# Gate weights laid out in memory by groups of expert blocks instead of blocks of tokens

## The chip, the cores and the metric

The kernel runs on one core of one Trainium2 chip. The metric is the device time of one execution in microseconds (us). The kernel before has a median of 3892.26 us over three runs (3888.90 to 3899.44 us).

## The reference, cut to what matters

Two layers, each with a token mixer, a cross-attention and a product-key expert layer (PEER); 512 tokens, 1024 channels. The change lies in the PEER layer: 16384 single-neuron experts, of which each token uses 128 (8 heads, the best 16 of each).

```
idx   = (e1 * 128 + e2)                # 128 experts a token
gates = softmax(vals)                  # their weights
ub  = peer_u[idx];  act = gelu(einsum('tkd,td->tk', ub, x))
vb  = peer_v[idx];  out = einsum('tk,tkd->td', gates * act, vb)
```

## The kernel before, in words

For 384 of the 512 tokens (TD) the kernel computes all experts densely and weights them by a gate that is zero for an expert that the token did not choose. The 16384 experts are 128 blocks (j) of 128 (n), and a group (GRP) is 8 blocks. The other 128 tokens fetch their own 128 rows of U and of V with indirect DMAs of GpSimd (`rows` L779, `rv` L795), in the same two stages:

- Stage U: for each block j a 128x1024 weight `w` is loaded (L198), split into a rounded part `wh` (ScalarE, L200) and a rest `wl` (VectorE, L202), and 24 matmuls of 384 columns give `acc` (L216 to L218). Its Gelu goes to `ag` and, four blocks at a time, to `acts` in memory (L1029). The last two groups stay in the core. Meanwhile the routing of the tokens is worked out, and for every 4 tokens `spread` and `collect` make a 128 (expert n) x 128 (block j) table of gates in PSUM and copy it into `stage`. A stage holds 16 tokens (TB): on each partition n, 128 blocks x 16 tokens of float32. When it is full it is written to `gd` (printed `gates`, L994 and L997): 24 writes of 1 MB a layer.
- Stage V: the blocks are taken by groups, the last group first. At a group's first block, the gates `gg` of the whole group are loaded (L807, 24 token blocks x 8 blocks x 16 tokens on each partition, 1.5 MB), then the activations `ar` of the group (L1058, 1.5 MB). The loads for a group are called for ahead, as soon as the buffer of that parity is free: two buffers of each. Then per block: `wv` = activation x gate (VectorE, L1062), its split `ws` (L222, L223), and 24 matmuls into eight accumulators `out` in PSUM. The first group's gates have a place of their own, `big`, and are loaded at the end of stage U, after all 24 writes have landed.

All loads and stores but the indirect ones are issued by SyncE in program order, on one queue (q1). GpSimd's are on another (q0). `w` has 4 buffers (WB), `wh` 3 (HB), `wl` 3 (LB); `stage` 2; `rows` 3 and `rv` 4. The order of the instructions on each engine follows the program's generators (`routes`, `scatter`, `rows_u`, `rows_v`), which are advanced by fixed credits for each block.

In memory, `gd` before is [24 token blocks, 128 n, 128 j, 16 tokens]. A stage is 8192 contiguous bytes on each partition, so a write is 128 packets of 8192 bytes. A group's gates are, for each n and token block, 8 x 16 x 4 = 512 contiguous bytes, so a read is 3072 packets of 512 bytes, 1 MiB apart from one token block to the next.

Of the kernel before, what the change touches and what calls it, by code (L numbers as in the profile page):

```python
# [10 lines left out]
F32 = mybir.dt.float32  # L11
# [14 lines left out]
NK = 128  # L26
# [6 lines left out]
TB = 16  # L33
TD = 384
NTB = TD // TB
# [15 lines left out]
GRP = 8  # L51
# [102 lines left out]
def trunk(ctx: ExitStack, tc: tile.TileContext, A, out, dbg=None):  # L154
    nc = tc.nc
# [13 lines left out]
    @contextmanager  # L169
    def tpool(**kw):  # L170
        if kw.get("space") == bass.MemoryType.DRAM:
            with tc.tile_pool(**kw) as pool:
                yield pool
        else:
            with tc.tile_pool(reuse_waits="tile", **kw) as pool:
                yield pool if kw.get("space") == PS else Lines(pool)
# [5 lines left out]
    dram = ctx.enter_context(tpool(name="dram", bufs=1, space=bass.MemoryType.DRAM))  # L182
# [577 lines left out]

    def peer(l):
        acts = dram.tile([NK // GRP, 128, GRP, TD], F32, name=f"acts{l}")
        gd = dram.tile([NTB, 128, NK, TB], F32, name=f"gates{l}")
        NG = T // 128 - TD // 128
        left = ExitStack()
        gp = left.enter_context(tpool(name=f"pg{l}", bufs=1))
# [36 lines left out]
        gates = {}  # L803

        def gate_group(pool, name, g):
            gg = pool.tile([128, NTB, GRP, TB], F32, name=name)
            nc.sync.dma_start(gg, gd[:, :, g * GRP:(g + 1) * GRP, :].rearrange("b p j t -> p b j t"))  # L807
            return gg

        with tpool(name=f"pr{l}", bufs=1) as rt, tpool(name=f"ph{l}", bufs=1) as hp, tpool(name=f"pps{l}", bufs=4, space=PS) as psum, \  # L810
# [132 lines left out]
            def spread(t0):  # L943
                parts = t0 // 4 % GVM < GVN
                dt = F32R if parts else F32
                oh = pp.tile([128, 8, NK], dt, name="oab", bufs=2)
                nc.vector.tensor_tensor(oh, C("iota")[:, None, :].to_broadcast([128, 8, NK]),  # L947
                                        pe[:, t0:t0 + 4].rearrange("p t e -> p (t e)")[:, :, None]
                                        .to_broadcast([128, 8, NK]), op=OP.is_equal)
                ob = pp.tile([128, 4, 2, NK] if parts else [128, 4, 1, NK], dt, name="ob", bufs=2)  # L950
                for i in range(4):
                    for k in ((0, 1) if parts else (2,)):
                        nc.scalar.activation(ob[:, i, k % 2], oh[:, 2 * i + 1].bitcast(F32), AF.Copy,  # L953
                                             scale=pg[:, k, t0 + i:t0 + i + 1])
                return oh, ob, parts

            def collect(t0, oh, ob, parts, stage):
                dst = stage[:, :, t0 % TB:t0 % TB + 4]
                if parts:
                    for h in range(2):  # L960
                        g = psm.tile([128, 2, 2, NK], F32, name="sm")
                        for i in range(2):
                            nc.tensor.matmul(g[:, i], lhsT=oh[:, 4 * h + 2 * i], rhs=ob[:, 2 * h + i], start=True,  # L963
                                             stop=True)
                        d = dst[:, :, 2 * h:2 * h + 2]
                        nc.scalar.copy(d, g[:, :, 0].rearrange("p t n -> p n t"))
                        nc.vector.tensor_add(d, g[:, :, 1].rearrange("p t n -> p n t"), d)
                else:
                    g = psm.tile([128, 4, NK], F32, name="sm")
                    for i in range(4):  # L970
                        nc.tensor.matmul(g[:, i], lhsT=oh[:, 2 * i], rhs=ob[:, i, 0], start=True, stop=True)  # L971
                    nc.scalar.copy(dst, g.rearrange("p t n -> p n t"))

            routed = [False] * TT

            def routes():
                for t in RORD:
                    yield from route(t)
                    routed[t] = True

            def scatter():
                for t in range(TD // 128):
                    pend = None
                    for t0 in range(t * 128, (t + 1) * 128, 4):
                        while not routed[t]:
                            yield
                        if t0 % TB == 0:
                            stage = pp.tile([128, NK, TB], F32, name="stage", bufs=2)
                        cur = (t0,) + spread(t0) + (stage,)
                        yield  # L990
                        if pend:
                            collect(*pend)
                            if t0 % TB == 0:
                                nc.sync.dma_start(gd[t0 // TB - 1], pend[-1])  # L994
                        pend = cur
                    collect(*pend)
                    nc.sync.dma_start(gd[(t + 1) * 128 // TB - 1], pend[-1])  # L997
                gates[NK // GRP - 1] = gate_group(gp, "big", NK // GRP - 1)

            rows = rows_u() if NG else iter(())  # L1000
            todo, groups = routes(), scatter()
            last = []
            rc = gc = xc = 0.0
# [37 lines left out]
        with tpool(name=f"pv{l}", bufs=1) as vp, tpool(name=f"vps{l}", bufs=1, space=PS) as psum:  # L1041
            acc = [psum.tile([128, T], F32, name=f"out{c}") for c in range(DC)]
            pend = []
# [8 lines left out]
            for j in v_order():  # L1052
                g, i = divmod(j, GRP)
                if i == 0:
                    gg = gates.get(g) or gate_group(vp, f"gg{g % 2}", g)
                    if j < NK - GC * GRP:
                        ar = vp.tile([128, GRP, TD], F32, name=f"ar{(g + 1) % 2}")
                        nc.sync.dma_start(ar, acts[g])  # L1058
                kept = j - (NK - GC * GRP)
                act = ar[:, i] if kept < 0 else last[kept // 4][:, i % 4]  # L1060
                wv = vp.tile([128, TD], F32, name="wv", bufs=2)
                nc.vector.tensor_mul(wv.rearrange("p (b t) -> p b t", b=NTB),  # L1062
                                     act.rearrange("p (b t) -> p b t", b=NTB), gg[:, :, i, :])
                ws = vp.tile([128, 2, TD], F32R, name="ws", bufs=max(3, NCM))
                split(ws, wv)
                pend.append((weights("v", l, j, ahead=1 if j == GRP - 1 else 2), ws))
                if not GRP - NCM <= j < GRP:
                    products(j, pend.pop())
                credit += VPACE
                while credit > 0:  # L1070
                    credit -= next(todo, VPACE)
# [12 lines left out]
    for l in range(L):  # L1084
        kvs = ExitStack()
        mixer(l, kvs)
        cross(l, kvs)
        kvs.close()
        peer(l)
# [74 lines left out]
```

## Time and profile before

| | |
|---|---|
| median of three runs | 3892.26 us |
| the profiled execution | 3897.86 us |
| span of that execution, first to last instruction | 3896.0 us |
| TensorE busy | 3811.9 us, 98% |
| VectorE, ScalarE, GpSimd busy | 77%, 49%, 19% |
| mean granted clock of TensorE | 0.992 |
| moved by DMA | 877.06 MB, mean 225 GB/s |
| stage U of the two layers | about 818 to 1380 and 2757 to 3320 us |
| stage V of the two layers | about 1389 to 1940 and 3328 to 3881 us |

The profile is of one execution, in microseconds from the first instruction. A busy TensorE is a modelled figure: a matmul's listed length overlaps the next one's start, so the distance between starts says more than the length. A wait named in the tables is the idle time of an engine and what ended it. A DMA's "time to landing" is counted from its issue on the queue to the last byte's semaphore. The share of the DMA engines in a window is the sum of the packets' lengths over 16 engines, which can pass 100% where packets overlap.

### The profile page before, as it was taken

How to read it: one execution, taken by the hardware profiler on the slowest of the kernel's cores; microseconds unless marked ns; L12 is line 12 of the kernel's file. 1: busy time of each engine (PE TensorE's matmuls, PEld its weight loads, DVE VectorE, ACT ScalarE, POOL GpSimd, SP SyncE). 2: the span in 40 equal slices, each digit the busy share in tenths (PEclk: the TensorE clock that was granted, in tenths of full speed). 3: DMA queues.
4: the chain of work that ended last, by engine and by line, in shares of the span. 5: the costliest groups of instructions: out<-in, count | busy, mean ns of one | idle time of the engine just before them, and what ended most of it. 6: DMA issues, size and time to landing. Idle time of an engine off the chain costs nothing.

```text
span 3896.0 us, 56299 instructions
## 1 busy us (share of the span) xinstructions
PE 3811.9 (98%) x20636; PEld 3540.7 (91%) x20636; DVE 3000.8 (77%) x5556; ACT 1901.9 (49%) x3531; POOL 757.3 (19%) x517
## 2 busy tenths in 40 slices
PE   8999999999999999999999999999999999999998
PEld 7888887899999999999978888878999999999998
DVE  7449665999989868777754596659999898687877
ACT  5336444336778833333343363543367788333333
POOL 0000000023233223443100000000232332233432
PEclk9999999999999999999999999999999999999999
DMA  4222232268889899999722223312788998999995
GB/s 148 81 92 92 103 130 71 87 229 307 313 319 353 310 315 345 334 333 340 253 81 76 92 93 108 130 67 87 246 311 304 332 349 302 325 347 326 333 323 216
DMA packets 315523, 877.06 MB, mean 225 GB/s; under 512 B 24944, under 2 KB 131568, under 8 KB 305264
## 3 DMA queue, kind: packets, MB, share of 16 engines
q1 hardware_dynamic: 241520, 605.01, 43.5%
q0 software_dynamic: 73728, 268.47, 19.6%
q8 instruction: 162, 2.65, 0.3%
q14 instruction: 113, 0.93, 0.1%
HBM read 776.13 MB, written 97.26 MB: 224 GB/s over the span
## 4 chain that ended last, share of the span: by engine, by line
PE 71%; DVE 13%; DMA 11%; issue 3%; ACT 1%; SPq 1%; POOL 0%; DVEq 0%; ACTq 0%; POOLq 0%
PE acc L216 17%; PE acc L218 17%; PE acc L217 17%; DMA w<-peer_v 8%; PE out L216 5%; PE out L217 4%; PE out L218 4%; DVE wl L202 4%; DMA rows<-peer_ur,irow 2%; PE sm L971 2%; PE sm L963 1%; DVE wk L837 1%; SPq L1058 1%; DVE idx L839 1%; DVE idx L836 1%
## 5 line engine op out<-in xcount | busy, mean ns | idle before, releaser
L200 ACT CAST wh<-w 128x1024 fp32r<-128x1024 f32 x768 | 802.5, 1049 | 1101.2 <-PE acc L217 661.1
L202 DVE TENSOR_TENSOR wl<-w,wh 128x1024 fp32r<-128x1024 f32 x768 | 936.4, 1220 | 398.4 <-ACT wh L200 375.1
L779 POOL DMA_INDIRECT rows<-peer_ur,irow x256 | 359.6, 1404 | 2358.2 <-DVE irow L927 1686.4
L216 PE MATMUL acc<-hf,wh 128*128 128x384 f32 (+1 forms) x2256 | 777.4, 345 | 8.5 <-DVE hf L223 6.1
L218 PE MATMUL acc<-hf,wl 128*128 128x384 f32 (+1 forms) x2256 | 775.7, 344 | 7.2 <-DVE wl L202 7.1
L217 PE MATMUL acc<-hf,wh 128*128 128x384 f32 (+1 forms) x2256 | 774.1, 343 | 0.0
L216 PE MATMUL out<-ws,wh 128*128 128x384 f32 x2048 | 693.9, 339 | 35.5 <-ACT wh L200 18.9
L217 PE MATMUL out<-ws,wh 128*128 128x384 f32 x2048 | 689.6, 337 | 0.0
L218 PE MATMUL out<-ws,wl 128*128 128x384 f32 x2048 | 576.6, 335 | 0.0
L795 POOL DMA_INDIRECT rv<-peer_v,irow x256 | 397.4, 1552 | 733.5 <-DVE yrow L800 608.9
L216 PE MATMUL acc<-a,wh 128*128 128x512 f32 x1280 | 506.2, 396 | 15.9 <-ACT wh L200 10.5
L217 PE MATMUL acc<-a,wh 128*128 128x512 f32 x1280 | 504.0, 394 | 0.0
L218 PE MATMUL acc<-a,wl 128*128 128x512 f32 x1280 | 503.0, 394 | 0.0
L216 PEld LDWEIGHTS acc<-hf,wh 128*128 128x128 f32 x2256 | 425.4, 189 | 19.5 <-DVE hf L223 8.7
L218 PEld LDWEIGHTS acc<-hf,wl 128*128 128x128 f32 x2256 | 425.0, 188 | 18.1 <-DVE wl L202 10.0
L217 PEld LDWEIGHTS acc<-hf,wh 128*128 128x128 f32 x2256 | 425.5, 189 | 7.7
L216 PEld LDWEIGHTS out<-ws,wh 128*128 128x128 f32 x2048 | 388.7, 190 | 41.9 <-ACT wh L200 24.8
L217 PEld LDWEIGHTS out<-ws,wh 128*128 128x128 f32 x2048 | 389.0, 190 | 0.0
L953 ACT ACTIVATE ob<-oab,pg 128x128 fp32r<-128x128 f32 (+1 forms) x1152 | 357.2, 393 | 43.2 <-DVE oab L947 42.7
L218 PEld LDWEIGHTS out<-ws,wl 128*128 128x128 f32 x2048 | 376.7, 189 | 0.0
L222 ACT CAST ws<-wv 128x384 fp32r<-128x384 f32 x256 | 131.0, 512 | 502.4 <-PE out L218 270.9
L782 DVE SCALAR_TENSOR_TENSOR prod<-rows,hrow 128x1024 f32<-128x1024 f32 x256 | 311.9, 1218 | 44.9 <-DMA rows<-peer_ur,irow 44.0
(291 smaller groups left out, 5218.5 us busy)
## 6 DMA issues: line engine op xcount, KB each, us to landing
w<-peer_u SPq DMA_DIRECT2D x256, 512.0 KB, 5.6
w<-peer_v SPq DMA_DIRECT2D x256, 512.0 KB, 6.0
gates<-stage SPq DMA_DIRECT2D x48, 1024.0 KB, 6.7
gg<-gates SPq DMA_DIRECT2D x30, 1536.0 KB, 14.6
acts<-ag SPq DMA_DIRECT2D x56, 768.0 KB, 5.8
ar<-acts SPq DMA_DIRECT2D x28, 1536.0 KB, 18.1
w<-w_f SPq DMA_DIRECT2D x80, 512.0 KB, 3.3
w<-w_t SPq DMA_DIRECT2D x32, 512.0 KB, 3.3
```

Source lines behind the costliest of these rows:

```text
L200: nc.scalar.copy(wh, w)
L202: nc.vector.tensor_sub(wl, w, wh.bitcast(F32))
L216: nc.tensor.matmul(acc, lhsT=lh, rhs=rl, start=start, stop=False)
L217: nc.tensor.matmul(acc, lhsT=lh, rhs=rh, start=False, stop=False)
L218: nc.tensor.matmul(acc, lhsT=ll, rhs=rh, start=False, stop=stop)
L222: nc.scalar.copy(dst[:, 0], src)
L779: nc.gpsimd.indirect_dma_start(out=r, out_offset=None, in_=A["peer_ur"].rearrange("l e d -> (l e) d"), in_offset=bass.IndirectOffsetOnAxis ...
L782: nc.vector.scalar_tensor_tensor(s, r, 1.0, hrow, op0=OP.mult, op1=OP.mult, accum_out=arow[:, k:k + 1])
L795: nc.gpsimd.indirect_dma_start(out=r, out_offset=None, in_=pv, in_offset=bass.IndirectOffsetOnAxis(ap=irow[:, 1, k:k + 1], axis=0))
L836: nc.vector.max_index(idx[:, 0:8], v[:, 0:8], src)
L953: nc.scalar.activation(ob[:, i, k % 2], oh[:, 2 * i + 1].bitcast(F32), AF.Copy, scale=pg[:, k, t0 + i:t0 + i + 1])
L971: nc.tensor.matmul(g[:, i], lhsT=oh[:, 2 * i], rhs=ob[:, i, 0], start=True, stop=True)
```

## The change

`gd` becomes [16 groups, 128 n, 24 token blocks, 8 j, 16 tokens]. A group's gates are now 24 x 8 x 16 x 4 = 12288 contiguous bytes on each partition: a read is 128 packets of 12288 bytes. A stage is now written as 16 pieces of 512 bytes on each partition, one into each group's part: 2048 packets of 512 bytes, 1.5 MiB apart from one group to the next. The bytes moved, the tiles in the core, the waits and the order of the instructions on all five engines are the same as before; only the shapes of the 48 writes and 32 reads differ (SyncE's row `gates<-stage 128x2048` becomes `128x16x128`, `gg<-gates 128x24x128` becomes `128x3072`).

```
-        gd = dram.tile([NTB, 128, NK, TB], F32, name=f"gates{l}")
+        gd = dram.tile([NK // GRP, 128, NTB, GRP, TB], F32, name=f"gates{l}")
...
         def gate_group(pool, name, g):
             gg = pool.tile([128, NTB, GRP, TB], F32, name=name)
-            nc.sync.dma_start(gg, gd[:, :, g * GRP:(g + 1) * GRP, :].rearrange("b p j t -> p b j t"))
+            nc.sync.dma_start(gg, gd[g])
             return gg
...
+            def put(b, stage):
+                nc.sync.dma_start(gd[:, :, b].rearrange("g p j t -> p g j t"),
+                                  stage.rearrange("p (g j) t -> p g j t", j=GRP))
...
                             if t0 % TB == 0:
-                                nc.sync.dma_start(gd[t0 // TB - 1], pend[-1])
+                                put(t0 // TB - 1, pend[-1])
                         pend = cur
                     collect(*pend)
-                    nc.sync.dma_start(gd[(t + 1) * 128 // TB - 1], pend[-1])
+                    put((t + 1) * 128 // TB - 1, pend[-1])
```

## Rows read from the trace of the kernel before

**Rows 1.** Busy time by stretch: stage U, stage V of the first layer

```profile
core 0: us, PE busy (x) PEld busy (x) DVE busy (x) ACT busy (x) POOL busy (x), PEclk, DMA share, GB/s
818.00:1369.00 551.00, 546.64 (x3331) 545.23 (x3330) 506.00 (x906) 396.84 (x978) 180.84 (x129) 1.00 0.87 315
...
1388.00:1900.00 512.00, 502.18 (x2851) 499.31 (x2852) 401.41 (x482) 174.53 (x238) 190.28 (x121) 0.99 0.94 333
```

**Rows 2.** TensorE's waits in stage U, first layer: total us, times, longest us

```profile
PE acc L218 <- DVE wl L202: 2.8, 2, 1.8
```

**Rows 3.** TensorE's waits, end of U and stage V, first layer

```profile
PE out L216 <- DVE ws L223: 8.7, 1, 8.7
PE out L216 <- ACT wh L200: 8.6, 8, 3.0
```

**Rows 4.** The same of the second layer

```profile
PE out L216 <- ACT wh L200: 10.4, 9, 2.8
PE out L216 <- DVE ws L223: 7.7, 1, 7.7
```

**Rows 5.** Chain of waits in stage V: start us, us, what

```profile
1683.46 15.11 DMA w<-peer_v
```

**Rows 6.** TensorE's instructions around one of these waits: start, us, what, [idle before]

```profile
1869.70 0.34 PE L218 MATMUL out<-ws,wl 128*128 128x384 f32 x1
1872.99 0.69 PE L216 MATMUL out<-ws,wh 128*128 128x384 f32 x1 [2.96 <-ACT wh L200]
```

**Rows 7.** Busy time by stretch, ahead of that wait and behind it

```profile
1860.00:1869.50 9.50, 9.50 (x56) 9.50 (x56) 5.50 (x8) 1.03 (x2) 1.01 (x1) 1.00 1.02 412
1873.00:1878.00 5.00, 5.00 (x16) 5.00 (x17) 5.00 (x6) 1.31 (x2) 1.01 (x1) 0.50 0.37 125
```

**Rows 8.** SyncE's queue, start of V and one group in V: start, us on it

```profile
1379.14 11.54 SPq L807 DMA_DIRECT2D gg<-gates  x2
...
1643.29 0.38 SPq L807 DMA_DIRECT2D gg<-gates  x1
1643.72 4.87 SPq L1058 DMA_DIRECT2D ar<-acts  x1
```

**Rows 9.** Chain of waits from stage U to stage V, first layer, then second

```profile
1368.84 5.09 DMA gates<-stage
1373.99 12.46 DMA big<-gates
...
3308.70 4.79 DMA gates<-stage
3313.55 11.76 DMA big<-gates
```

**Rows 10.** DMA windows 1388:1396 (gg), 1399:1404.5 (ar), 1370:1371.3 and 1370:1373 (gates)

```profile
DMA packets 4544, 2.33 MB, mean 291 GB/s; under 512 B 17, under 2 KB 4541, under 8 KB 4544
...
DMA packets 215, 2.33 MB, mean 423 GB/s; under 512 B 17, under 2 KB 26, under 8 KB 26
...
DMA packets 69, 0.56 MB, mean 429 GB/s; under 512 B 1, under 2 KB 1, under 8 KB 1
...
DMA packets 131, 0.94 MB, mean 313 GB/s; under 512 B 10, under 2 KB 10, under 8 KB 23
```

**Rows 11.** DMA queues, 1381 to 1383 us: packets, MB, share

```profile
q0 software_dynamic: 184, 0.68, 86.3%
q1 hardware_dynamic: 176, 0.11, 18.1%
```

**Rows 12.** DMA issues of the page: count, KB each, median us to landing

```profile
gates<-stage SPq DMA_DIRECT2D x48, 1024.0 KB, 6.7
...
mem<-memT SPq DMA_DIRECT2D x2, 1024.0 KB, 5.5
```

**Rows 13.** Time to landing: gg; then w in U, first and second layer

```profile
DMA to landing us min/median/max: 11.2/14.6/20.2
...
DMA to landing us min/median/max: 3.1/6.3/9.6
...
DMA to landing us min/median/max: 3.2/6.1/11.6
```

## The prediction

> **What bounds the kernel now.** I read first the busy time by stretch, then TensorE's waits stage by stage, then the chain of waits where they stand, and last the DMA view of short windows in which a single kind of transfer runs.
>
> TensorE is the engine that sets the time, and it hardly ever stops: in stage U it is busy for 546.6 of 551 us, in stage V for 502 of 512 [rows 1]. So only its few stops can be won, and they are easily counted. In U they are 2.8 us in two waits for `wl`, before the first write of gates [rows 2]. In V they are, in the first layer, one wait of 8.7 us at the start and eight of 8.6 us together; in the second, one of 7.7 and nine of 10.4 [rows 3, 4]. All but the first wait for a `wh`, and the chain shows what that `wh` waited for: the load of a V weight that took some 15 us to land [rows 5]. That weight is issued behind a group's gates and activations, 3 MB on the same queue. The wait of 8.7 us is the turn from U to V: the last write of gates must land (5.09 us), then `big` is read (12.46 us), then the first product can be formed [rows 9].
>
> Both stages use the DMA engines hard: a share of 0.87 at 315 GB/s in U and 0.94 at 333 GB/s in V [rows 1].
>
> **The change part by part.** No instruction moves; the packets of the 48 writes and 32 reads change size. So I price packets, from windows in which they run nearly alone [rows 10]: gates in packets of 512 bytes come at 291 GB/s, activations in packets of 12288 bytes at 423 GB/s, and the writes in packets of 8192 bytes go at 429 GB/s for the first 1.3 us and 313 GB/s over 3 us.
>
> *A read of a group's gates in V.* 1.57 MB takes 5.4 us at 291 GB/s and 3.7 us at 423. That frees 1.7 us of the queue in each group. There is a second gain. Behind the 3072 packets the queue's next issue is held: 4.87 us for the `ar` of one group, and 11.5 us for two gate reads in a row [rows 8]. The new read has 128 packets. I reckon when the late weight would land. Before, it lands about 20 us after the issue of `gg` (15.1 us after its own issue [rows 5], which the hold put off by some 5). After: 3.7 for `gg`, 3.7 for `ar`, 1.3 for the weight ahead, 1.3 for itself (0.52 MB at 423 each), 3.0 of fixed delay (`mem`, 1.05 MB, lands in 5.5 us, of which 2.5 are bytes at 423 [rows 12]), and up to 3.2 for two gathers of GpSimd that share the engines: 13 to 16 us. That is 4 to 7 us earlier, and the longest wait is 3.0. So I take all of these waits as gone: 8.6 + 10.4 = 19.0 us. Each also costs a refill that the table does not count: two starts lie 3.29 us apart where the listed wait is 2.96 and the usual distance 0.17, so 0.16 more [rows 6]; 17 waits, 2.7 us. After that wait of 2.96 us the granted clock was 0.50, the lower level, and 16 matmuls took 5.0 us, where 56 took 9.5 before it [rows 7]: 16 x (0.31 - 0.17) = 2.3 us. Three of the waits are of that length (3.0 in the first layer, and by their sum I take two in the second), about 2 us each: 6 us. V gives 19.0 + 2.7 + 6 = 27.7 us. What is late next there: nothing that I find; TensorE at its pace of 0.17 us a matmul.
>
> *The turn from U to V.* `big` needs 3.7 us of bytes and 3.0 of fixed delay, 6.7 instead of 12.46 and 11.76 us [rows 9]. Part of the old time was the gather: between 1381 and 1383 the two queues sent almost as many packets each (184 and 176), of 4096 and of 512 bytes, so that the gates got 18% [rows 11]. A read of eight packets an engine is over before that gather starts at all. The write ahead gets slower: 1.05 MB at 291 GB/s takes 3.6 us, against 2.4 to 3.35 now. The trace has no write in packets of 512 bytes, so this is a bound from reads: +0.25 to +1.2, I take +0.8. From the other side: `gg` took 11.2 to 20.2 us to land [rows 13], and two thirds of its packets would be 7.5 to 13.5 us, against a median of 6.7 for a write now [rows 12]: at worst +6.8. I stay by the 291, because it is the only row of packets of this size running alone. So 12.46 - 6.7 - 0.8 = 5.0 and 11.76 - 6.7 - 0.8 = 4.3, together 9.3 us. The waits of 8.7 and 7.7 do not vanish; some 3.5 us of each stay, enough for the clock to fall as it does now, so I gain nothing on the clock there.
>
> *The writes in U.* 24 a layer, each 0.8 us longer on a queue that has room: at 315 of 423 GB/s a quarter of 551 us, some 140 us, is spare, and 24 x 0.8 is 19. What can cost is a weight `w` queued behind a write. It lands after 6.3 us in the median and after 9.6 and 11.6 at most [rows 13]. In V a landing of 15.1 us gives a wait of about 1 us, so about 14 us are tolerated (four buffers, some 4 us of matmuls each). A write's 0.8 and a hold of the queue behind its 2048 packets, under the 4.87 us that stood behind 3072 and which I put at 3, bring the worst to 15.4 and the median to 10. I charge 1 us in all, and keep 10 us for the upper end.
>
> A gather's `rows` that share the engines with a write fare better than now, since small packets alternate with theirs [rows 11]; nothing is charged or gained, as TensorE does not wait for them.
>
> The sum: 27.7 + 9.3 - 1 = 36.0 us. From the profiled execution's 3897.86 us that gives 3861.9. That execution lies 5.6 us above the median of the runs, so from the median it is 3856.
>
> **A rule of the skill against a row.** The rows put packets of 512 bytes at 291 GB/s, at 0.69 of the large ones [rows 10]. The Trainium skill, "DMA: Bandwidth & Descriptors", section Specifications, says a transfer reaches line rate from 512 bytes on. By that rule neither the reads nor the writes would change at all; the trace does not agree with it. The same page, in Latency and other measured facts, warns of rows a large power of two apart in memory: 164 GB/s at a pitch of 2 MiB, 103 at 4 MiB. The new write steps by 1.5 MiB, and an estimate from that page would be 6.4 to 10.2 us a write. The trace is against it so far: the reads of before step by 1 MiB and ran at 291 GB/s. No row shows it for writes.
>
> **The rivals.**
>
> *Slow writes: slower than before.* Each write in 512-byte pieces, scattered 1.5 MiB apart, takes 6.8 us longer, the upper bound above. Then 24 writes need 163 us where 140 are spare: 23 us a layer, and with weights that land at 13 us in the median and TensorE stopped at the later ones, I put 30. That is +60; the turn gives nothing (12.46 - 6.7 - 6.8 is below zero), V still gives 27.7: +32, 3924 us. It turns to a loss from about (140 + 14) / 24 = 6.4 us a write. For it: no write of this form is in the trace, and memory may treat scattered writes otherwise than reads. Against it: the read with a like stride at 291 GB/s. Chance 0.09.
>
> *U takes a part back.* The writes are 2 to 4 us longer, or hold the queue, and some weights land past 14 us: 10 to 15 us a layer. 3880 us, chance 0.07.
>
> *The queue's order is what makes the weight late.* `gg` and `ar` still stand before it with 3 MB, and VectorE's chain takes the place of the load. Then only the turn gains: 9.3 - 1 = 8, 3884 us. For it: 7.4 us of bytes stay ahead of the weight. Against it: 4 to 7 us gained where the longest wait is 3.0. Chance 0.07.
>
> *Nothing changes*, because small packets cost no more where other traffic fills the engines (the rule on 512 bytes above would be its reason): 3892 us, chance 0.04.
>
> **How the numbers follow.** The forecast has 0.73. Low end: the write +0.25, `big` at 5.5 us (the landing of 1 MB), 6.7 + 6.0 at the turn, all of V: 40 us, and the runs of before spread 10 us, of which I allow some: 3843. High end: half of V's waits stay (-14), the turn gives 4, U takes 10: 3884. It takes in the two middle rivals and leaves out most of the slow writes. What differs by under 0.3%, 11.7 us, can't be told from no change. Faster by more: 0.73, most of the U rival, a little of the third: 0.80. Within it: the rest of the third and the fourth and some of the second, 0.11. Slower: 0.09.
>
> **What would show it.** Right: `gg` lands in about 7 us or less ahead of other loads, SyncE's issue of `ar` behind it takes under 1 us, TensorE's waits for `wh` in V are gone, `big` lands in 6 to 7 us, and the wait at the turn is 3 to 4 us. Wrong: a write lands in over 10 us in the median; TensorE waits in U for `wl` or `wh` behind the first write; or `wh` in V still waits for `w`.

## The result and the profile after

The changed kernel takes 3855.14 us (median of four runs, 3851.76 to 3855.58), the one before 3895.37 (four runs as well). The ratio is 0.9894, with a 95% interval of 0.9878 to 0.9909: faster by 1.1%. A second series of runs gave 0.9882 (0.9865 to 0.9900). The profiled execution took 3855.28 us, with a span of 3853.2, 42.8 less than before.

TensorE's waits after, in the order of the two layers: first the turn and stage V of the first layer, then of the second, then stage U of the first. Columns as in [rows 2 to 4].

```profile
PE out L216 <- DVE ws L223: 2.7, 1, 2.7
...
PE out L216 <- DVE ws L223: 3.6, 1, 3.6
...
PE acc L218 <- DVE wl L202: 3.2, 2, 2.3
```

All 17 waits for `wh` of [rows 3, 4] are gone; only the turn is left, a third to a half of what it was, and U is much as it was [rows 2] (those rows leave out a wait of 1.2 us for `wh` and one of 0.4 us that stood in U before). The same is read from the busy time by stretch, to be held against [rows 1]:

```profile
818.00:1369.00 551.00, 547.80 (x3340) 546.77 (x3339) 506.29 (x907) 397.65 (x978) 180.80 (x129) 1.00 0.92 316
...
1388.00:1900.00 512.00, 512.00 (x2956) 512.00 (x2955) 416.66 (x497) 180.63 (x248) 181.25 (x124) 1.00 0.90 341
```

In V TensorE is busy for the whole of the 512 us, with the same share of the DMA engines or less. In U the share rose from 0.87 to 0.92 at the same bytes: the price of the small writes, for which TensorE does not wait. It is 0.92 with the writes alone changed and 0.88 with the reads alone (both runs below).

The chain of waits at the turn, first layer and second, against [rows 9]:

```profile
1367.22 5.11 DMA gates<-stage
1372.39 6.31 DMA big<-gates
...
3285.53 5.56 DMA gates<-stage
3291.15 6.81 DMA big<-gates
```

The read takes a little over half its old time; the write took 0.0 and 0.8 us longer. Over all issues after, count, KB and median us to landing, against 6.7 and 14.6 before [rows 12, 13]:

```profile
gates<-stage SPq DMA_DIRECT2D x48, 1024.0 KB, 8.6
gg<-gates SPq DMA_DIRECT2D x30, 1536.0 KB, 9.0
```

Where the 42.8 us come from: TensorE's first and last matmul of stage V in both layers, before, then after (a row's first number is its start).

```profile
1389.16 0.69 PE L216 MATMUL out<-ws,wh 128*128 128x384 f32 x1 [8.74 <-DVE ws L223]
...
1940.13 0.34 PE L218 MATMUL out<-ws,wl 128*128 128x384 f32 x1
...
3328.02 0.69 PE out L216
...
3880.74 0.34 PE L218 MATMUL out<-ws,wl 128*128 128x384 f32 x1
```

```profile
1381.49 0.69 PE L216 MATMUL out<-ws,wh 128*128 128x384 f32 x1 [2.69 <-DVE ws L223]
...
1917.28 0.34 PE L218 MATMUL out<-ws,wl 128*128 128x384 f32 x1
...
3300.68 0.69 PE L216 MATMUL out<-ws,wh 128*128 128x384 f32 x1 [3.56 <-DVE ws L223]
...
3837.62 0.34 PE L218 MATMUL out<-ws,wl 128*128 128x384 f32 x1
```

From first start to last, V of the first layer took 551.0 us and now takes 535.8: 15.2 less. The second goes from 552.7 to 536.9, 15.8 less. Together 31.0. The turn is 10.1 us shorter (8.7 + 7.7 against 2.7 + 3.6). The 1.7 that remain lie ahead of the turn of the first layer, where nothing was forecast: the first matmul of V starts 7.7 us earlier, and the turn accounts for 6.0 of them.

### The profile page after: what moved, and what is told of

It reads as the page before. It is cut to its first block, busy times and chain, and to the rows that moved or that the text cites. A ratio compares the mean times of both kernels' runs of the same rounds, so it can differ in the third digit from the quotient of the medians.

```text
span 3853.2 us, 56299 instructions
## 1 busy us (share of the span) xinstructions
PE 3801.3 (99%) x20636; PEld 3535.2 (92%) x20636; DVE 2999.6 (78%) x5556; ACT 1900.1 (49%) x3531; POOL 734.3 (19%) x517
## 4 chain that ended last, share of the span: by engine, by line
PE 88%; DVE 8%; DMA 2%; issue 1%; ACT 1%; POOL 0%; SPq 0%; DVEq 0%; ACTq 0%; POOLq 0%
PE acc L216 18%; PE acc L218 18%; PE acc L217 18%; PE out L216 9%; PE out L217 9%; PE out L218 9%; PE sm L971 2%; DVE wl L202 2%; DMA rows<-peer_ur,irow 1%; PE sm L963 1%; DVE wk L837 1%; DVE idx L839 1%; DVE idx L836 1%; DVE val L838 1%; DVE val L835 1%
## 5 line engine op out<-in xcount | busy, mean ns | idle before, releaser
L795 POOL DMA_INDIRECT rv<-peer_v,irow x256 | 373.0, 1457 | 716.6 <-DVE yrow L800 609.7
L953 ACT ACTIVATE ob<-oab,pg 128x128 fp32r<-128x128 f32 (+1 forms) x1152 | 357.2, 393 | 38.6 <-DVE oab L947 37.7
L800 DVE SCALAR_TENSOR_TENSOR yrow<-rv,wrow,yrow 128x1024 f32<-128x1024 f32 x254 | 324.5, 1278 | 50.9 <-DMA rv<-peer_v,irow 50.9
```

What stands on the lines that cost most here:

```text
L795: nc.gpsimd.indirect_dma_start(out=r, out_offset=None, in_=pv, in_offset=bass.IndirectOffsetOnAxis(ap=irow[:, 1, k:k + 1], axis=0))
L800: nc.vector.scalar_tensor_tensor(yrow, r, wrow[:, k:k + 1], yrow, op0=OP.mult, op1=OP.add)
```

## The experiments

**Reads alone and writes alone.** The two halves of the change, each with the other half as before. The gates then lie in the wrong places, which changes their values and not the work.

```
# reads_only: written as before, read as 12288 contiguous bytes a partition
+ flat = gd.rearrange("b p j t -> (b p j t)").rearrange("(g p x) -> g p x", g=NK // GRP, p=128)
+ nc.sync.dma_start(gg.rearrange("p b j t -> p (b j t)"), flat[g])
# writes_only: written as after, read in pieces of 512 bytes
+ flat = gd.rearrange("g p b j t -> (g p b j t)").rearrange("(b p j t) -> b p j t", b=NTB, p=128, t=TB)
+ nc.sync.dma_start(gg, flat[:, :, g * GRP:(g + 1) * GRP, :].rearrange("b p j t -> p b j t"))
```

> Only the reads are changed: gates are written as before (128 packets of 8192 bytes) and read as 128 packets of 12288 bytes; the gates then lie in the wrong places, so the output is not the reference's. Theory (the whole gain comes from the reads, in V and at the turn, and the 512-byte writes are hidden in U): 3853 to 3858 us, the same as the changed kernel within 3 us, no wait of TensorE for wh in V, turn of 3 to 4 us a layer. Rival (the new writes themselves help, since gathers get more of the DMA engines beside small packets, or the write order makes U end earlier): 3862 us or more. Rival (the new writes cost something in U or at the turn that the reads pay for): 3850 us or less.

> Only the writes are changed: 2048 packets of 512 bytes each, while a group's gates are still read as 3072 packets of 512 bytes (from the wrong places, so the output is not the reference's). Theory (writes are hidden in U): the time of the kernel before, 3890 to 3899 us, with 17 or so waits for wh in V of 19 us together and a turn of 8 to 9 us a layer. Rival (slow writes): over 3905 us, with waits of TensorE in U for wl or wh. Rival (small writes help U): under 3888 us.

Measured: reads alone 3852.47 us, ratio 0.9879 (0.9859 to 0.9900); writes alone 3899.26 us, 1.0006 (0.9994 to 1.0017). The waits, writes alone, first layer:

```profile
PE out L216 <- ACT wh L200: 12.1, 9, 2.9
PE out L216 <- DVE ws L223: 8.0, 1, 8.0
```

The whole gain is the reads'; the writes cost nothing that can be measured. Both times lie a few tenths of a microsecond outside the theory's ranges (3853 to 3858, 3890 to 3899), in a series in which the kernel before took 3899.94 us; by the ratios both are as the theory had it. The waits for `wh` in V, put at 19 us in the two layers, were 24.3 in the profiled execution with the writes alone changed.

**Twice the writes.** Each write of gates made a second time, into memory that nobody reads: once in 2048 packets of 512 bytes, once in 128 of 8192.

```
+ g2 = dram.tile([NK // GRP, 128, NTB, GRP, TB], F32, name=f"copy{l}")
 def put(b, stage):
     nc.sync.dma_start(gd[:, :, b]...)
+    nc.sync.dma_start(g2[:, :, b].rearrange("g p j t -> p g j t"), stage.rearrange("p (g j) t -> p g j t", j=GRP))
# copy_large, instead: g2 = [NTB, 128, NK * TB]
+    nc.sync.dma_start(g2[b], stage.rearrange("p j t -> p (j t)"))
```

> The changed kernel with each of the 48 writes of gates made a second time, in the same 2048 pieces, into memory that nobody reads. Theory (U's DMA queue has about 140 us to spare a layer, and 24 more writes at 3.6 us are 86): TensorE's waits in U grow by under 5 us a layer; the copy of the last write stands ahead of the turn's read, 2 to 4 us more a layer: 3858 to 3868 us. Rival (a weight behind a write is near the edge of lateness already, so each further microsecond is paid by TensorE): 1 us or more for each of the 24, 3880 to 3910 us.

> The kernel write_twice with its second write made in 128 packets of 8192 bytes instead of 2048 of 512; the instructions of the engines stand in the same order in both, and in another than in the changed kernel. Theory (write_twice lost its 38 us to that other order, which the compiler's planner chose when it saw 48 more transfers, and not to the packets): within 4 us of write_twice, 3889 to 3897 us, with the same stops of TensorE in the same places. Rival (the packets of the writes weigh on U): 8 us or more less than write_twice, 3860 to 3885 us.

write_twice took 3893.00 us (ratio 0.9981, 0.9971 to 0.9990), 38 more than the changed kernel: the theory's 3858 to 3868 missed, and the rival's range hit. But the rival's reason was wrong too. The compiler's planner, which orders the instructions, had put them in another order on TensorE, VectorE, ScalarE and GpSimd. copy_large has that same order on all four, and took 3892.28 us with the same stops. TensorE's waits in stage V, then in U, of the first layer; the three lines are the same, digit for digit, in write_twice and in copy_large:

```profile
PE out L216 <- ACT wh L200: 6.4, 4, 1.6
PE out L218 <- DVE wl L202: 3.0, 2, 2.1
...
PE acc L216 <- ACT wh L200: 4.1, 6, 1.7
```

Not one of these waits feels that 24 writes a layer went in 16 times as many packets. So even at twice the writes U does not pay for packets of 512 bytes. The pair alone leaves open whether the 38 us are the order's or those of 24 MB more a layer, since both runs have both. The traces speak for the order: in V nothing is copied, and 9.4 us a layer of these waits stand there; and of the 14 waits of over 0.3 us in U and V of the first layer, behind the first writes, each was ended by an instruction of ScalarE or VectorE that ran straight behind another one of its own engine and had not waited for a load. A kernel in that order without the copies was not run.

**Pieces between 512 and 12288 bytes.** Two or four token blocks side by side, so that a group is read in pieces of 1024 or 2048 bytes. Writes and order are the changed kernel's.

```
-gd = dram.tile([NK // GRP, 128, NTB, GRP, TB], ...)
+gd = dram.tile([NK // GRP, NTB // 2, 128, 2, GRP, TB], ...)      # read2048: 4 for 2
-nc.sync.dma_start(gg, gd[g])
+nc.sync.dma_start(gg.rearrange("p (c k) j t -> p c (k j t)", k=2), gd[g].rearrange("c p k j t -> p c (k j t)"))
```

> The changed kernel with a group's gates in pieces of 1024 bytes: two token blocks side by side, read as 1536 packets; the writes stay at 2048 packets of 512 bytes, and the order of instructions is that of the changed kernel. Theory (the weights were late because the 3072 packets held the queue's next issues for 5 us; fewer packets end that): the hold behind the gate read is under 1.5 us, TensorE's waits for wh in V are nearly gone, 3854 to 3862 us. Rival (the bytes' pace on the DMA engines made them late; at 1024 bytes it is some half way between 291 and 423 GB/s): half of the waits in V and some of the turn are back, 3868 to 3882 us.

> The same with pieces of 2048 bytes, 768 packets. Theory (hold): as the changed kernel, 3853 to 3858 us. Rival (pace): 3858 to 3866 us, the turn 0.5 to 1 us longer a layer and a wait or two in V.

1024 bytes: 3877.77 us, ratio 0.9943 (0.9927 to 0.9958). 2048 bytes: 3863.08 us, 0.9914 (0.9899 to 0.9929). Both are in the rival's range and not in that of the theory. With 2048 bytes the profiled execution, the fastest of four at 3858.71 us, has no wait for `wh` in V and turns of 4.4 and 4.2 us. With 1024 the turns are 5.5 and 9.0 us, so not all of its loss lies in V. The row of `ar`'s issue on SyncE's queue gives the hold behind the gate read (min/median/max in ns), before and with 1024 bytes; then TensorE's waits in V with 1024 bytes, first and second layer:

```profile
L1058 SPq DMA_DIRECT2D ar<-acts x28: 433/5296/10007, 1390.8 to 3794.9; - x28
```

```profile
L1063 SPq DMA_DIRECT2D ar<-acts x28: 433/1516/5048, 1384.2 to 3775.9; - x28
...
PE out L216 <- ACT wh L200: 5.7, 6, 2.9
...
PE out L216 <- ACT wh L200: 4.9, 7, 1.5
```

The hold fell from 5.3 to 1.5 us, and more than half of the waits stayed (10.6 of 19.0 us). With 2048 bytes it is 0.7 us in the median and in the changed kernel 0.6, and still a group's bytes need 2.6 us more with 2048, as the lengths below show. So the hold was not the main thing that made the weights late: while SyncE is held, the DMA engines work on what is queued (their share is 69% for q1 and 33% for q0 in the first window below). What did is seen in windows that run from the issue of a `gg` to the end of the last packet of its `ar`, for one group each of before, of 1024 bytes and after (18.1, 16.9 and 12.9 us long); columns are packets, MB and share:

```profile
q1 hardware_dynamic: 3551, 4.34, 69.3%
q0 software_dynamic: 642, 2.34, 33.1%
```

```profile
q1 hardware_dynamic: 2027, 4.39, 70.0%
q0 software_dynamic: 587, 2.15, 31.8%
```

```profile
q1 hardware_dynamic: 494, 3.92, 76.7%
q0 software_dynamic: 339, 1.26, 24.3%
```

Ahead of the late weight stand the group's 3 MB and whatever of GpSimd's gathers gets in between. With small packets 2.34 MB of gathers pass, with large ones 1.26. The reading is that the two queues take turns by packets, and that a packet of 512 bytes is a small turn: in [rows 11] 176 of them went beside 184 of the gather. Over the groups of both layers the medians of the length, here to the start of that last packet, are 18.0, 17.0, 15.6 and 13.0 us (512, 1024, 2048 and 12288 bytes), with 555, 528, 435 and 306 gather packets of 4096 bytes ahead; at 159 ns, the commonest length of such a packet, on one of 16 engines these are 5.5, 5.2, 4.3 and 3.0 us. So by this estimate 2.5 of the 5.0 us gained are gathers that now wait their turn and 1.7 the pace of the bytes (5.4 us less 3.7). The 0.8 that are left may be q1's own bytes: in these stretches its median fell from 4.13 to 3.86 MB, 0.6 us at 423 GB/s.

That the turns cause it is read from these counts; no kernel was run that changes the turns alone in V. In U, though, the runs part them, since there only the packets of the writes differ. VectorE's waits for gathered `rows` add up to 44.0 and 41.3 us where gates are written in packets of 8192 bytes (before, reads_only), and to 27.9 and 31.5 us with packets of 512 (after, writes_only): beside small packets the gather comes sooner.

**The turn taken away.** In early_big 23 of the 24 token blocks of the first group are read before the last write, and the last is copied inside the core. In early_ws the first block's product and split are moved into U as well (`wv` in the place of `pe`, `ws` in that of `prod`).

```
+nc.sync.dma_start(gg[:, 0:NTB - 1], gd[g][:, 0:NTB - 1])        # ahead of the last collect
 collect(*pend)
+nc.sync.dma_start(gg[:, NTB - 1].rearrange("p j t -> p (j t)"), pend[-1][:, g * GRP:].rearrange("p j t -> p (j t)"))
# early_ws, in stage U at block 124
+nc.vector.tensor_mul(wv..., last[2][:, 0]..., gates[g][:, :, 0, :])
+split(first_ws[0], wv)
```

> The changed kernel with the first group's gates read ahead: 23 of its 24 token blocks are loaded before the last write of gates, and the last block is copied from the stage inside the core, so that the turn from U to V waits neither for the last write nor for the large read. Theory (the 3.0 and 3.9 us between U's last and V's first matmul are this chain alone): these gaps go, and the half clock behind them too, about 10 matmuls at 0.32 instead of 0.17 us, 1.5 us a layer: 7 to 10 us less than the changed kernel, 3845 to 3848 us. Rival (a weight of V or VectorE's split is late there anyway): the gap stays at 2 us or more and the time is 3851 to 3856 us.

> early_big with the first block's product of activation and gate, and its split, made inside stage U, ahead of the last weights' splits in the queues of ScalarE and VectorE. Theory (with the load gone, the 3.0 us at the turn were left because that split stood behind a cast of a weight whose buffer only U's last matmul frees): the gap falls under 1 us and TensorE's clock stays up: 3 us a layer and 1 to 1.5 us of slow matmuls, 3842 to 3848 us. Rival (something else stands there, as the release of the PSUM accumulators): the gap stays at 2.5 to 3 us, 3851 to 3855 us. Rival (the split waits for the gates and keeps later weights waiting in ScalarE's queue): 3855 us or more.

early_big: 3852.16 us, ratio 0.9877 (0.9856 to 0.9897), in the rival's range. Its chain at the turn of the first layer has no DMA in it any more, and is as long as the changed kernel's:

```profile
1379.73 1.05 ACT wh L200
...
1380.81 1.22 DVE wl L202
1382.03 0.48 DVE ws L223
...
1382.56 0.44 PE out L216
```

A cast of a V weight needs a `wh` buffer that U's last matmul gives back at 1379.7; the split of the first product stands behind it. From U's last start to V's first it is 3.0 us in both layers here, against 3.0 and 3.9 in the changed kernel. So 3.0 us of the turn were already a queue's order and not the load. (The order differs a little in this run too, in 630 of VectorE's 5556 places.) early_ws took the gap to 0.17 us, as its theory had it, and still lost: 3866.58 us (0.9923, 0.9910 to 0.9937). Products of the gathered `rows` that stood in U now stand in V (68 of VectorE's instructions on `prod` in each layer, none in the changed kernel), presumably because the first block's split holds the buffer of `prod`. TensorE waits there again:

```profile
PE out L217 <- ACT wh L201: 8.8, 5, 2.4
```

**early_big beside the changed kernel.**

> early_big once more, beside the changed kernel on the same chip: 2 to 4 us below it, 3850 to 3855 us, since its two gaps at the turn were 3.0 and 3.0 us against 3.0 and 3.9. Rival: within 1 us of it, the turn being bound by the cast that only U's last matmul frees.

> The changed kernel once more, as the measure for early_big and pitch2m: 3852 to 3858 us.

3854.62 against 3855.73 us, both with the ratio 0.9882 (0.9865 to 0.9900). The 1.1 us between them are near the rival's 1 and short of the 2 to 4 expected: no difference to be measured. No kernel here is shown to beat the changed one.

**Writes made slow.** The gates spread so that neighbouring partitions lie 2 MiB apart.

```
-gd = dram.tile([NK // GRP, 128, NTB, GRP, TB], F32, name=f"gates{l}")
+gd = dram.tile([128, NK // GRP, 32768], F32, name=f"gates{l}")[:, :, 0:NTB * GRP * TB] \
+    .rearrange("p g (b j t) -> g p b j t", b=NTB, j=GRP)
```

> The changed kernel with its gates spread in memory: the rows of two neighbouring partitions lie 2 MiB apart instead of 12 KiB; packets, bytes and the order of instructions are the same. The Trainium skill, DMA: Bandwidth & Descriptors, Latency and other measured facts, gives 164 GB/s for copies at this pitch. If the reads then run at under 300 GB/s in 12288-byte packets, pace and hold come apart in stage V. Theory (the hold of the queue and the alternation of small packets with the gathers made the weights late): no hold, no wait for wh in V, V stays at 536 to 538 us; the turn gets 2 to 5 us longer and U may lose some: 3860 to 3880 us. Rival (pace): the waits for wh in V come back, 8 us or more a layer, over 3880 us. If the reads keep 400 GB/s, the pitch does not matter here and the time is 3851 to 3858 us.

3882.13 us, ratio 0.9954 (0.9939 to 0.9969), in the rival's "over 3880", but not by its way: V did not change at all (500 of 500 us busy between 1400 and 1900). The reads stayed fast enough, so pace and hold were not parted by this run. What got slow is the write. The chain at the turn, first layer, then two waits in U of the first layer:

```profile
1374.15 8.79 DMA gates<-stage
...
1383.00 9.37 DMA big<-gates
...
PE sm L972 <- ACT ob L954: 3.4, 3, 1.7
...
DVE prod L783 <- DMA rows<-peer_ur,irow: 37.7, 30, 4.5
```

The last packet of a write ends 10.8 us after its issue in the median, against 8.1 in the changed kernel (later in 44 of the 48 writes). From first start to last U is 7.5 and 6.0 us longer, and the turn 6.7 and 6.0 us (9.3 and 9.6 against 2.7 and 3.6): the 26 us by which this kernel is slower than the changed one. In U the loss does not come through the weights. VectorE waits 37.7 us for gathered `rows`, against 9.3 in the same window of the changed kernel, and TensorE then waits for `ob` of ScalarE, which follows VectorE's work. At 1356.6 the chain runs from a gather of 8.7 us over `prod` and `oab` to `ob`. So this is the forecast's rival of slow writes, brought about on purpose, with another path in U than the one that was priced.

The Trainium skill ("DMA: Bandwidth & Descriptors", Latency and other measured facts) gives 164 GB/s for copies at a pitch of 2 MiB between partitions. The trace agrees in direction only: a write at 1364.4 with no gather beside it took 4.9 us from its first packet to its last, with 0.3 MB of weights among them, against 3.6 us for the same write of the changed kernel, where 164 GB/s would make it 6.4. The prediction's 6.4 to 10.2 us a write, worked out from the same row, were for a step of 1.5 MiB between groups; in the changed kernel neighbouring partitions lie 12 KiB apart, and no slowing of this size is seen there.

## Why the prediction was right

The forecast was 3856 us, the median 3855.14. By its steps:

- *What bounds the kernel, and the count of stops.* Right: the waits that there were to win were 19.0 us in V and 16.4 at the turn [rows 3, 4], and all of V's went.
- *V, 27.7 us.* 31.0. The waits were exact. The part around them, refill and clock, was put at 8.7 and was 12.0. Behind the three long waits the clock cost about what was taken, 5.8 against 6 us. But each wait costs some 0.27 us of refill and not the 0.16 that I read from one start to the next, since the second matmul behind it is late as well. And the half clock behind the turn is shorter in the first layer (3.1 us from 1381.5 instead of 5.4 from 1389.2), which gives back 1 us; in the second it is as long as before (5.6 instead of 5.3).
- *Why the weight lands earlier.* The size was right (4 to 7 us; 5.0 at the last packet of `ar`, and 4.6 at the landing of the weight behind it, 21.2 and now 16.6 us after the issue of `gg` in the median), the reason half wrong. I gave the second part of the gain to the queue's hold; read1024 took most of the hold away and more than half of the waits stayed. The step that failed took time in which an issue waits for time in which the DMA engines stand idle. What gave the rest, as far as the counts show, is the share of the engines that the gathers took while the gates came in small packets. The forecast had seen this at the turn [rows 11] and did not carry it into V. One of its signs did not show: `gg` was to land in about 7 us or less, and took 9.0 in the median and 7.9 at least. The other signs came: `ar` is issued in 0.6 us, `big` lands in 6.3 and 6.8, the waits at the turn are 2.7 and 3.6.
- *The turn, 9.3 us.* 10.1. `big` at 6.7 was 6.3 and 6.8; the write's +0.8 was 0.0 and 0.8. That the clock would fall there all the same was right: half of full speed from 1381.5 on (0.53 granted between 1381 and 1384.4).
- *The writes in U, a cost of 1 us.* None, though they were slower than forecast. Over the 48 writes the landing took 8.6 us in the median against 6.7, 1.9 and not 0.8 longer. The issue behind a write, held for 3 us by the forecast, took 1.9 us in the median and 6.8 at most (0.3 and 1.2 before). And the room of 140 us that was taken from the bytes is 72 us a layer by the busy share of 0.87 in the same row. A `w` landed after 13.5 and 14.0 us at most, close to the 14 that I took as tolerated; TensorE did not wait once more for it.

The *slow writes* did not come, since a 512-byte write running alone took about as long as one of large packets (below). pitch2m shows that the rival was priced too low: there the writes end some 2 us later, not 6.8, and U already loses 13.5 us in the two layers, by way of the gathers, for which the forecast charged nothing. *U takes a part back* met its condition, writes about 2 us longer and a held queue, but not its price. *The queue's order* fell with the waits in V, and *nothing changes* with the time.

That the forecast is 1 us off is luck. The sum of 36.0 us is 6.8 short of the 42.8 between the two profiled spans: 3.3 in V, 0.8 at the turn, 1 in U and 1.7 ahead of the first turn. Against that stood the 5.6 us that I took off because the profiled execution of before lay that far above its median. With a fourth run that median is 3895.37, only 2.5 below, and the profiled execution of after lies at its own median.

## What to carry to other kernels

Of two sides of a transfer one can have the large packets: give them to the side that someone waits for, and the small ones to the side whose queue is ahead of its use. Where two DMA queues run at once, count packets as well as bytes: in the counts here, many small packets left more of the engines to the other queue. And when a variant adds an instruction, compare the order on every engine before its time is put down to the thing added; here 38 us went with a reordering and looked like the very effect that was tested.

## What was not expected of the hardware

A write to memory in packets of 512 bytes, with hardly a gather beside it, takes about as long as one in large packets: from first packet to last 3.2 to 4.3 us for the last two writes of each layer after, 3.1 to 3.9 before. The last write of the first layer after, between 1368.5 and 1371 us, running alone:

```profile
DMA packets 1701, 0.87 MB, mean 348 GB/s; under 512 B 0, under 2 KB 1701, under 8 KB 1701
```

That is 348 GB/s, against 313 to 429 for packets of 8192 bytes and 291 for reads of 512 [rows 10].

But the small packets are not free on the engines, and there reads and writes are alike. The median length of a packet on q1 is 27, 46, 84, 309 and 460 ns for 512, 1024, 2048, 8192 and 12288 bytes, and the 27 ns hold for the gates read before as for the gates written after. A write of 2048 such packets keeps all 16 engines for 3.5 us instead of 2.5. Twenty-four of them are 23 us more a layer, which is the rise of the share in U from 0.87 to 0.92.
